# One copy of the bias rows for both halves, byte masks, later small loads, and an output in pieces

## The chip, the cores and the metric

The kernel runs on one core of a Trainium2 chip. The metric is device time in microseconds for one execution. Before the change the median of three runs is 849.18 us (849.12 to 850.76). All engine times below come from one further execution, recorded by the hardware profiler: it took 852.8 us, of which 851.0 us lie between its first and its last instruction (the span).

The engines are PE (TensorE, the matmuls), DVE (VectorE), ACT (ScalarE), POOL (GpSimd) and SP (SyncE, which here only issues DMAs).

## The reference, cut to what matters

Two blocks run on 256 tokens of width 1024 (16 "meta" tokens stand ahead of them in the first block, which makes 272 rows).

```python
a = rms_norm(h, norm_mix)
(q_na, k_na, v_na, q_hg, z_f, z_b, i_hg, g_hg, gate_na, gate_hg) = split_cols(a @ w_in)
y_na  = neighbourhood_attention(q_na, k_na, v_na, rpb) @ w_na_out     # 8 heads, bias table rpb (8 x 15 x 31)
y_hg  = hgrn2_branch(q_hg, z_f, z_b, i_hg, g_hg, lb, hg_norm) @ w_hg_out   # two gated scans
h = h + (sigmoid(gate_na) * y_na + sigmoid(gate_hg) * y_hg) @ w_o
h = h + square(relu(rms_norm(h, norm_mlp) @ w_up)) @ w_down
x = rms_norm(h, norm_final)[:, 16:]
# second block, two layers:
ada = silu(c) @ ada_w + ada_b                 # shift, scale, gate; ada_w is 1024 x 3072 per layer
x = x + gate * ((mixers of (rmsnorm(x) * (1 + scale) + shift) @ in_w) * silu(gate2)) @ out_w
out = rmsnorm(x, final_g)                     # 256 x 1024
```

In the neighbourhood attention a grid row of 64 tokens sees a window of 16 columns, and the bias of a query and a key is an entry of `rpb` that depends on their distance alone. The scans use seven binary masks of 128 x 128 (`lvl`).

## The kernel before

All weights are fp32 and are multiplied in three passes: a weight is split into a rounded high part and the rest. Weights come in 129 "units" of 512 x 512 (1 MB), in the order in which PE uses them: `gh` (units 0 and 1), `kn` (2 and 3), `qn` (4 and 5), `vn` (6 and 7) and so on. `emit_raw` loads a unit (L222, on SP's queue) into one of three `raw` buffers. `emit_hl` splits it in two halves: ACT writes `whi` (L252), DVE then writes `wlo` = raw - whi (L253, two SBUF inputs). There are six pairs of half-unit buffers. A raw buffer is free again when DVE has split its second half; a `whi`/`wlo` pair is free when PE has read it last.

PE accumulates in four PSUM banks (`acc`). `gh` uses two. `kn` uses four, one for each 128 columns (L357 to L359), and `qn` uses the same four again: qn's first matmul can start only when the first of kn's results has been copied out of its bank (`ev_kn`: ACT L647 or DVE L649, and a last DVE copy L651).

`bias_loads` builds the bias of the attention for two halves of the grid. For each half four DMAs (L622) fetch rows of `rpb` into a tile `braw`, and 12 additions on POOL (L627) add the window mask, which lies in `cs` (a constant, loaded at L584); both inputs lie in SBUF. `lvf` (448 KB of fp32, L586) is cast to bytes by POOL (L587) to give the masks `lvl`. `ada()` loads `ada_w` in 48 pieces of 512 KB (L457, issued by POOL) into four slots and multiplies them on DVE (L473, two operations each). At the end `ev_oo` normalizes the last rows: half by ACT (L1648), half by DVE (L1650), each with its own output DMA.

A scheduler that runs ahead of time with its own model of costs sets the order of the instructions on each engine. `with after(x):` tells it to issue what follows behind x. Each queue executes its instructions in that order; an instruction that waits holds all behind it on its engine.

Of the kernel before, what the change touches and what calls it, by code (L numbers as in the profile page):

```python
# [7 lines left out]
F32 = mybir.dt.float32  # L8
# [3 lines left out]
AF = mybir.ActivationFunctionType  # L12
ALU = mybir.AluOpType
# [14 lines left out]


C_LV = 0  # L30
C_ID = 896
C_WIN = C_ID + 128
C_GLA = C_WIN + 80
C_CUM = C_GLA + 128
# [7 lines left out]
def consts():  # L42
    import numpy as np

    c = np.zeros((128, C_N), np.float32)
    p = np.arange(128)
    c[:, C_ID:C_ID + 128] = np.eye(128)
    for i in range(7):

        a, b = p[:, None] >> i, p[None, :] >> i  # L50
        c[:, 128 * i:128 * i + 128] = (a ^ b) == 1
    for hf in (0, 1):
        col = 32 * hf + 31 - p % 32
        key = 24 * hf + np.arange(40)
        s = np.clip(col - 8, 0, 48)
        ok = (key[None, :] >= s[:, None]) & (key[None, :] < s[:, None] + 16)
        c[:, C_WIN + 40 * hf:C_WIN + 40 * hf + 40] = np.where(ok, 0.0, -1e30)
    t = np.arange(128)

    c[:, C_GLA:C_GLA + 128] = p[:, None] <= t[None, :]  # L60

    c[:, C_CUM:C_CUM + 128] = ((p[:, None] <= t[None, :]) & (p[:, None] // 64 == t[None, :] // 64)) / 16.0
    for g, w in enumerate((2, 4, 8, 16)):
        c[:, C_RC + 16 * g:C_RC + 16 * g + 16] = 1.0 / np.minimum(np.arange(16) + 1, w)
    return c
# [3 lines left out]
def kernel(  # L69
# [5 lines left out]
    vecs, cst, out, dbg=None,  # L75
):
    nc = tc.nc
    V, S, T, G = nc.vector, nc.scalar, nc.tensor, nc.gpsimd
# [17 lines left out]
    def mt(i, shape, dt=F32, name="m"):  # L96
        return slot.tile(shape, dt, name=nm(name), tag=f"m{i}")
# [33 lines left out]
    cs = cp.tile([128, C_N - C_WIN], F32, name="cs")  # L131
    lvl = cp.tile([128, 896], U8, name="lvl")
    vrow = cp.tile([128, 128], F32, name="vrow")
    vc = cp.tile([128, 128], F32, name="vc")
    h = [cp.tile([128, D], F32, name=f"h{t}") for t in range(2)]
# [67 lines left out]
            add_units(("oo", j, n), odd_out_w, 512 * j, 512 * n)  # L203

    raw_t, hl_t = {}, {}
    borrowed = {}
    cap = [1 << 30]
    BORROW = {("v0", 0): (("m8", "m9"), ("m10", "m11")), ("v0", 1): (("l0", "l1"), ("l2", "m18")),
# [5 lines left out]
    def emit_raw(n):  # L214
        while st["raw"] < min(n, len(units)):
            i = st["raw"]
            t = rawp.tile([128, 2048], F32, name=nm("raw"), tag="raw")
            src = units[i][1]
            d = t.rearrange("p (k n) -> p k n", n=src.shape[2])

            for k in (slice(0, 2), slice(2, 4)) if i < QD else (slice(None),):
                nc.sync.dma_start(out=d[:, k], in_=src[:, k])  # L222
            raw_t[i] = t
            st["raw"] += 1


    for key, tags in BORROW.items():
        i = [u[0] for u in units].index(key)
# [43 lines left out]
    def after(instructions):  # L272
        es = ExitStack()
        for ins in instructions:
            es.enter_context(tc.issue_after(ins.ins))
        return es
# [169 lines left out]
    def ada(l, js, slots):  # L446
        if 4 in js:
            gr[l] = mt(13 + l, [128, D], name="gr")
        parts = [(j, k2) for j in js for k2 in range(4)]
        ws = []  # L450

        def load(i):

            if i < len(parts):
                j, k2 = parts[i]
                w = slot.tile([128, 2, 512], F32, name=nm("adw"), tag=slots[i % len(slots)])
                nc.gpsimd.dma_start(out=w, in_=ada_w[l, 256 * k2:256 * k2 + 256, 512 * j:512 * j + 512]  # L457
                                    .rearrange("(k p) n -> p k n", p=128))
                ws.append(w)

        for i in range(len(slots)):
            load(i)
        i = len(slots)
        yield 3000
        for j in js:
            a = tb()
            G.memset(a, 0.0)
            nc.gpsimd.dma_start(out=a[0:1], in_=ada_b[l:l + 1, 512 * j:512 * j + 512])
            for k2 in range(4):
                w = ws.pop(0)  # L470
                for k in range(2):
                    kk = 2 * k2 + k
                    V.scalar_tensor_tensor(out=a, in0=w[:, k], scalar=csil[:, kk:kk + 1], in1=a,  # L473
                                           op0=ALU.mult, op1=ALU.add)
                load(i)
                i += 1
                yield 1200
            if j < 4:

                p2 = transposes(a).rearrange("p (k c) -> p k c", k=4)  # L480
                if j < 2:
                    V.tensor_reduce(out=cols[:, l, 8 + 4 * j:12 + 4 * j], in_=p2, axis=AX.X, op=ALU.add)
                else:

                    o = R_NG + 8 * l + 4 * (j - 2)
                    c = small([128, 4])
                    V.tensor_reduce(out=c, in_=p2, axis=AX.X, op=ALU.add)
                    V.scalar_tensor_tensor(out=cols[:, l, 4 * (j - 2):4 * (j - 2) + 4], in0=c, scalar=1.0,
                                           in1=vc[:, o:o + 4], op0=ALU.add, op1=ALU.mult)
            else:  # L490
                ps = mps()

                ah, al = tb(dt=F32R), tb(dt=F32R)
                split_bank(a, ah, al)
                T.matmul(ps, lhsT=ones_r, rhs=ah, start=True, stop=False)
                T.matmul(ps, lhsT=ones_r, rhs=al, start=False, stop=True)
                S.activation(out=gr[l][:, 512 * (j - 4):512 * (j - 4) + 512], in_=ps, func=AF.Copy)
            yield 100
# [77 lines left out]
    def ev_gh(t, ps):  # L576
# [4 lines left out]

    xstat_unit([("gh", 0), ("gh", 1)], xT, ev_gh)
    meta_in()
    nc.sync.dma_start(out=cs, in_=cst[:, C_WIN:])  # L584
    lvf = mt(8, [128, 896], name="lvf")
    nc.sync.dma_start(out=lvf, in_=cst[:, 0:896])  # L586
    G.tensor_copy(out=lvl, in_=lvf)  # L587
    pv = mps()
    T.transpose(out=pv[:, 0:128], in_=vrow, identity=ident)
    V.tensor_copy(out=vc, in_=pv[:, 0:128])  # L590
# [4 lines left out]
                    in0=vc[:, R_LB:R_LB + 16].rearrange("p (d l h) -> p d l h", d=2, l=2)[:, :, 0],  # L595
                    in1=vc[:, R_LB:R_LB + 16].rearrange("p (d l h) -> p d l h", d=2, l=2)[:, :, 1], op=ALU.subtract)
# [16 lines left out]
    bias = [lt(hf, [128, 8, 176], name=f"bias{hf}") for hf in range(2)]  # L613

    def bias_loads():
        for hf in range(2):
            raw = mt(10 + hf, [128, 8, 133], name="braw")
            for r in range(4):

                src = bass.AP(tensor=na_rpb.tensor, offset=na_rpb.offset + (7 - r) * 31 - 16 - 8 * hf,  # L620
                              ap=[[1, 32], [465, 8], [1, 133]])
                nc.sync.dma_start(out=raw[32 * r:32 * r + 32], in_=src)  # L622
            for hd in range(8):
                rv = raw[:, hd]
                for r0, n, o in KEYS[hd // 2 % 2][:-1]:
                    rows = bass.AP(tensor=rv.tensor, offset=rv.offset + 31 * r0, ap=[list(rv.ap[0]), [31, n], [1, 40]])
                    G.tensor_tensor(out=bias[hf][:, hd, o:o + 40 * n].rearrange("p (j c) -> p j c", j=n), in0=rows,  # L627
                                    in1=C(C_WIN + 40 * hf, 40).unsqueeze(1).to_broadcast([128, n, 40]), op=ALU.add)
                o = KEYS[hd // 2 % 2][-1]
                G.memset(bias[hf][:, hd, o:o + 16], 0.0)  # L630
            yield 0
# [372 lines left out]
    for n in range(2):  # L1004
        ws = use(("yn", n))
        for t in range(2):
# [3 lines left out]
            c = slice(512 * n, 512 * n + 512)  # L1010
# [3 lines left out]
    for n in range(2):  # L1014
        ws = use(("yh", n))
        nl = len(later)
        for t in range(2):
# [3 lines left out]
            c = slice(512 * n, 512 * n + 512)  # L1021
# [333 lines left out]
    for t in range(2):  # L1355
        for gp in range(2):
            ps = mps()
            for k in range(2):
                g = 2 * gp + k
                for c in range(2):  # L1360
                    i = 2 * g + c
# [121 lines left out]
    GA = {}  # L1483

    glw = cp.tile([128, 8, 16], F32, name="glw")
    nc.sync.dma_start(out=glw, in_=odd_in_w[:, 2048:2064].rearrange("(k p) n -> p k n", p=128))
    glr = cp.tile([128, 8, 32], F32R, name="glr")
    split_bank(glw, glr[:, :, 0:16], glr[:, :, 16:32])
    gw3 = slot.tile([33, 512], F32, name="gw3", tag="c0")
    nc.sync.dma_start(out=gw3[0:16], in_=gla_gate_w)  # L1490
    nc.sync.dma_start(out=gw3[16:32], in_=gla_gate_w)
    nc.sync.dma_start(out=gw3[32:33], in_=gla_gate_b)

    def gla_gate():
        pg = mps()
# [145 lines left out]
    def ev_oo(t, n, ps, a, b):  # L1641
        c = slice(512 * n + a, 512 * n + b)
        resid(1, t, n, ps, a, b)
        if n == 0:
            G.tensor_tensor(out=h[t][:, c], in0=h[t][:, c], in1=fg_b[:, c], op=ALU.mult)
        if n == 1 and b == 512:
            r = rpow(sqs[t])
            S.activation(out=h[t][:, 0:512], in_=h[t][:, 0:512], func=AF.Copy, scale=r)  # L1648
            nc.scalar.dma_start(out=out[128 * t:128 * t + 128, 0:512], in_=h[t][:, 0:512])
            V.scalar_tensor_tensor(out=h[t][:, 512:1024], in0=h[t][:, 512:1024], scalar=r, in1=fg_b[:, 512:1024],  # L1650
                                   op0=ALU.mult, op1=ALU.mult)
            nc.sync.dma_start(out=out[128 * t:128 * t + 128, 512:1024], in_=h[t][:, 512:1024])

    out_proj("oo", (2, 3, 0, 1), oT, ev_oo, halves=True)

# [44 lines left out]
```

## Time and profile before

| what | value |
|---|---|
| median of three runs | 849.18 us |
| the profiled execution | 852.8 us, span 851.0 us |
| PE busy | 829.6 us (97%) |
| DVE, ACT, POOL busy | 585.4, 463.9, 89.7 us |
| bytes read from HBM | 167.00 MB, 197 GB/s over the span |
| mean granted clock of PE | 0.996 |

A line of the timeline reads: start, duration (of the whole group where it says x2 or more), engine, source line, operation, result <- operands, shapes, and in brackets the idle time of the engine ahead of it with what ended it. A matmul's duration is longer than the distance to the next one, since matmuls overlap; the distance of two starts tells PE's pace.

### The profile page before, as it was taken

The numbers are of one execution on the slowest core, as the hardware profiler recorded it, in microseconds if no ns is written. First come the engines' busy times: TensorE is split into PE (matmuls) and PEld (weight loads), VectorE is DVE, ScalarE is ACT, GpSimd is POOL, SyncE is SP. The second block draws the span as 40 slices with busy tenths as digits, with TensorE's granted clock in tenths as the row PEclk, the third lists the DMA queues.
The fourth block names the chain that finished last, engine by engine and source line by source line (L and its number), as shares of the span: only waits on it lengthen the run. The fifth ranks groups of instructions, "written<-read, shape, count | busy, mean of one in ns | idle before, by whom it ended". The sixth has DMA issues, their size and how long they took to land.

```text
span 851.0 us, 12884 instructions
## 1 busy us (share of the span) xinstructions
PE 829.6 (97%) x5037; PEld 735.7 (86%) x5037; DVE 585.4 (69%) x838; ACT 463.9 (55%) x757; POOL 89.7 (11%) x188
## 2 busy tenths in 40 slices
PE   7799999999999999999999999999999999999996
PEld 4799998888889999999878988888789999888885
DVE  6756668764858887767976768966655557568743
ACT  6356755564557545545766545554566455455442
POOL 2400020001002221102021001100000000031001
PEclk9999999999999999999999999999999999999999
DMA  9874344441648998858737657856155445559611
GB/s 274 234 246 140 110 149 148 147 150 53 217 152 309 369 359 297 297 196 282 245 119 247 191 169 229 281 196 238 60 202 176 154 151 176 161 196 314 191 62 49
DMA packets 82832, 168.87 MB, mean 198 GB/s; under 512 B 4770, under 2 KB 9250, under 8 KB 82772
## 3 DMA queue, kind: packets, MB, share of 16 engines
q1 hardware_dynamic: 75188, 142.34, 49.8%
q0 software_dynamic: 7296, 25.19, 8.6%
q8 instruction: 39, 0.64, 0.3%
q10 hardware_dynamic: 288, 0.52, 0.2%
q14 instruction: 21, 0.17, 0.1%
HBM read 167.00 MB, written 1.05 MB: 197 GB/s over the span
## 4 chain that ended last, share of the span: by engine, by line
PE 90%; DVE 4%; DMA 2%; ACT 1%; issue 1%; POOL 0%; SPq 0%; POOLq 0%; ACTq 0%; DVEq 0%
PE acc L349 16%; PE acc L347 16%; PE acc L348 16%; PE acc L359 7%; PE acc L358 7%; PE acc L357 7%; PE mp L359 3%; PE mp L357 3%; PE mp L358 3%; PE mp L406 3%; DVE wlo L253 2%; PE mp L869 1%; DMA raw<-in_w_in_dram 1%; DMA h<-in_x_dram 1%; ACT junk L438 1%
## 5 line engine op out<-in xcount | busy, mean ns | idle before, releaser
L253 DVE TENSOR_TENSOR wlo<-raw,whi 128x1024 fp32r<-128x1024 f32 x244 | 297.7, 1240 | 136.2 <-ACT whi L252 133.8
L252 ACT ACTIVATE whi<-raw 128x1024 fp32r<-128x1024 f32 x244 | 251.2, 1055 | 170.0 <-PE acc L349 88.1
L473 DVE SCALAR_TENSOR_TENSOR tb<-adw,csil,tb 128x512 f32<-128x512 f32 x96 | 71.0, 747 | 8.2 <-DMA tb<-in_ada_b_dram 5.2
L359 PE MATMUL acc<-xh,wlo 128*128 128x272 f32 (+1 forms) x224 | 65.0, 292 | 4.6 <-DVE wlo L253 4.6
L358 PE MATMUL acc<-xl,whi 128*128 128x272 f32 (+1 forms) x224 | 65.1, 291 | 0.0
L357 PE MATMUL acc<-xh,whi 128*128 128x272 f32 (+1 forms) x224 | 64.9, 291 | 0.0
L357 PE MATMUL mp<-uh,whi 128*128 128x256 f32 x224 | 63.3, 284 | 0.0
L358 PE MATMUL mp<-ul,whi 128*128 128x256 f32 x224 | 63.2, 283 | 0.0
L359 PE MATMUL mp<-uh,wlo 128*128 128x256 f32 x224 | 62.3, 283 | 0.0
L457 POOL DMA_DIRECT2D adw<-in_ada_w_dram x48 | 35.2, 733 | 198.3 <-DVE tb L473 118.7
L359 PE MATMUL acc<-oh,wlo 128*128 128x256 f32 x192 | 55.0, 287 | 0.0
L358 PE MATMUL acc<-ol,whi 128*128 128x256 f32 x192 | 54.6, 284 | 0.0
L357 PE MATMUL acc<-oh,whi 128*128 128x256 f32 x192 | 54.4, 283 | 0.0
L347 PE MATMUL acc<-whi,hh 128*128 128x512 f32 x128 | 49.9, 391 | 0.0
L348 PE MATMUL acc<-wlo,hh 128*128 128x512 f32 x128 | 49.8, 390 | 0.0
L349 PE MATMUL acc<-whi,hl 128*128 128x512 f32 x128 | 49.7, 389 | 0.0
L347 PE MATMUL acc<-whi,yT 128*128 128x512 f32 (+1 forms) x128 | 48.5, 379 | 0.0
L348 PE MATMUL acc<-wlo,yT 128*128 128x512 f32 (+1 forms) x128 | 48.3, 378 | 0.0
L349 PE MATMUL acc<-whi,yT 128*128 128x512 f32 (+1 forms) x128 | 48.3, 377 | 0.0
L359 PEld LDWEIGHTS acc<-xh,wlo 128*128 128x128 f32 x224 | 42.6, 191 | 4.8 <-DVE wlo L253 4.8
L348 PE MATMUL acc<-wlo,oh 128*128 128x512 f32 x112 | 44.5, 398 | 0.0
L347 PE MATMUL acc<-whi,oh 128*128 128x512 f32 x112 | 44.2, 395 | 0.0
(415 smaller groups left out, 2053.2 us busy)
## 6 DMA issues: line engine op xcount, KB each, us to landing
raw<-in_odd_in_w_dram SPq DMA_DIRECT2D x28, 1024.0 KB, 5.2
adw<-in_ada_w_dram POOLq DMA_DIRECT2D x48, 512.0 KB, 6.2
raw<-in_w_in_dram SPq DMA_DIRECT2D x21, 1024.0 KB, 5.2
raw<-in_even_in_w_dram SPq DMA_DIRECT2D x20, 1024.0 KB, 5.2
raw<-in_w_up_dram SPq DMA_DIRECT2D x16, 1024.0 KB, 7.4
raw<-in_w_down_dram SPq DMA_DIRECT2D x16, 1024.0 KB, 8.5
raw<-in_even_out_w_dram SPq DMA_DIRECT2D x8, 1024.0 KB, 5.1
raw<-in_odd_out_w_dram SPq DMA_DIRECT2D x8, 1024.0 KB, 5.2
```

The source lines that it names most:

```text
L252: S.activation(out=hi.rearrange("p k n -> p (k n)"), in_=r, func=AF.Copy)
L253: V.tensor_tensor(out=lo.rearrange("p k n -> p (k n)"), in0=r, in1=f(hi.rearrange("p k n -> p (k n)")), op=ALU.subtract)
L347: T.matmul(ps, lhsT=xh, rhs=wh, start=first and k == 0, stop=False)
L348: T.matmul(ps, lhsT=xh, rhs=wl, start=False, stop=False)
L349: last_mm[:] = [T.matmul(ps, lhsT=xl, rhs=wh, start=False, stop=last and k == n - 1)]
L357: T.matmul(ps, lhsT=wh[:, c], rhs=xh, start=first and k == 0, stop=False)
L358: T.matmul(ps, lhsT=wh[:, c], rhs=xl, start=False, stop=False)
L359: T.matmul(ps, lhsT=wl[:, c], rhs=xh, start=False, stop=last and k == n - 1)
L406: last_t[:] = [T.transpose(out=ps[:, 128 * b:128 * b + 128], in_=src[:, 128 * b:128 * b + 128], identity=ident)]
L438: S.activation(out=j[0:src.shape[0], 0:n], in_=src, func=AF.Square, scale=float(of or n) ** -0.5, accum_out=a)
L457: nc.gpsimd.dma_start(out=w, in_=ada_w[l, 256 * k2:256 * k2 + 256, 512 * j:512 * j + 512] .rearrange("(k p) n -> p k n", p=128))
L473: V.scalar_tensor_tensor(out=a, in0=w[:, k], scalar=csil[:, kk:kk + 1], in1=a, op0=ALU.mult, op1=ALU.add)
```

## The change

1. The seven masks are stored as bytes in the constant and are loaded straight into `lvl` (112 KB instead of 448 KB). POOL's cast is gone.
2. The bias rows are loaded once for both halves: one tile for heads 0 to 3 and one for heads 4 to 7, each of four DMAs of 32 x 4 x 141 numbers (72 KB) in place of 32 x 8 x 133 (133 KB). The 24 additions stay the same, but half 0 now reads both tiles, and so does half 1; all 12 additions that read the first tile can stand ahead of the others.
3. The loads of `cs`, the bias rows, `lvl`, `glw` and `gw3` are issued behind the last weight load that was emitted before them (`after(raw_ins)`).
4. The 48 loads of `ada_w` go on SP's queue instead of POOL's.
5. DVE's half of the last output is computed and stored in two pieces of 256 columns.

```diff
-C_ID = 896
+C_ID = 224
...
+    masks = np.zeros((128, 896), np.uint8)
...
-        c[:, 128 * i:128 * i + 128] = (a ^ b) == 1
+        masks[:, 128 * i:128 * i + 128] = (a ^ b) == 1
+    c[:, C_LV:C_LV + 224] = masks.view(np.float32)
...
-                nc.sync.dma_start(out=d[:, k], in_=src[:, k])
+                raw_ins[:] = [nc.sync.dma_start(out=d[:, k], in_=src[:, k])]
...
-                nc.gpsimd.dma_start(out=w, in_=ada_w[l, 256 * k2:256 * k2 + 256, 512 * j:512 * j + 512]
+                nc.sync.dma_start(out=w, in_=ada_w[l, 256 * k2:256 * k2 + 256, 512 * j:512 * j + 512]
...
-    nc.sync.dma_start(out=cs, in_=cst[:, C_WIN:])
-    lvf = mt(8, [128, 896], name="lvf")
-    nc.sync.dma_start(out=lvf, in_=cst[:, 0:896])
-    G.tensor_copy(out=lvl, in_=lvf)
+
+    with after(raw_ins):
+        nc.sync.dma_start(out=cs, in_=cst[:, C_WIN:])
...
+        raw = [mt(10 + i, [128, 4, 141], name="braw") for i in range(2)]
+        with after(raw_ins):
+            for i in range(2):
+                for r in range(4):
+                    src = bass.AP(tensor=na_rpb.tensor, offset=na_rpb.offset + 4 * 465 * i + (7 - r) * 31 - 24,
+                                  ap=[[1, 32], [465, 4], [1, 141]])
+                    nc.sync.dma_start(out=raw[i][32 * r:32 * r + 32], in_=src)
+            nc.sync.dma_start(out=lvl.bitcast(F32), in_=cst[:, C_LV:C_LV + 224])
         for hf in range(2):
-            raw = mt(10 + hf, [128, 8, 133], name="braw")
-            for r in range(4):
-
-                src = bass.AP(tensor=na_rpb.tensor, offset=na_rpb.offset + (7 - r) * 31 - 16 - 8 * hf,
-                              ap=[[1, 32], [465, 8], [1, 133]])
-                nc.sync.dma_start(out=raw[32 * r:32 * r + 32], in_=src)
             for hd in range(8):
-                rv = raw[:, hd]
+                rv = raw[hd // 4][:, hd % 4, 8 - 8 * hf:]
...
-            V.scalar_tensor_tensor(out=h[t][:, 512:1024], in0=h[t][:, 512:1024], scalar=r, in1=fg_b[:, 512:1024],
-                                   op0=ALU.mult, op1=ALU.mult)
-            nc.sync.dma_start(out=out[128 * t:128 * t + 128, 512:1024], in_=h[t][:, 512:1024])
+            for k in range(2):
+
+                c = slice(512 + 256 * k, 768 + 256 * k)
+                V.scalar_tensor_tensor(out=h[t][:, c], in0=h[t][:, c], scalar=r, in1=fg_b[:, c],
+                                       op0=ALU.mult, op1=ALU.mult)
+                nc.sync.dma_start(out=out[128 * t:128 * t + 128, c], in_=h[t][:, c])
```

The scheduler makes a new order out of this. At the start of the program SP issues its loads so before the change (raw_227 is unit 3, raw_312, raw_374 and raw_448 are units 4, 5 and 6):

```order
L574 DMA hgn_b<-in_hg_norm_dram 128x512
L584 DMA cs<-in_cst_dram 128x400
L586 DMA lvf_291<-in_cst_dram 128x896
L622 DMA braw_483<-in_na_rpb_dram 32x8x133
L622 DMA braw_458<-in_na_rpb_dram 32x8x133 x2
L622 DMA braw_483<-in_na_rpb_dram 32x8x133
L622 DMA braw_458<-in_na_rpb_dram 32x8x133
L622 DMA braw_483<-in_na_rpb_dram 32x8x133
L622 DMA braw_458<-in_na_rpb_dram 32x8x133
L222 DMA raw_227<-in_w_in_dram 128x4x512
L622 DMA braw_483<-in_na_rpb_dram 32x8x133
L1486 DMA glw<-in_odd_in_w_dram 128x8x16
```

And so after it (raw_309, raw_371, raw_445 and raw_558 are units 4, 5, 6 and 7; braw_455 holds heads 0 to 3):

```order
L578 DMA hgn_b<-in_hg_norm_dram 128x512
L226 DMA raw_227<-in_w_in_dram 128x4x512
L590 DMA cs<-in_cst_dram 128x400
L226 DMA raw_309<-in_w_in_dram 128x4x512
L226 DMA raw_371<-in_w_in_dram 128x4x512
L226 DMA raw_445<-in_w_in_dram 128x4x512
L627 DMA braw_455<-in_na_rpb_dram 32x4x141 x4
L627 DMA braw_456<-in_na_rpb_dram 32x4x141 x4
L628 DMA lvl<-in_cst_dram 128x224
L226 DMA raw_558<-in_w_in_dram 128x4x512
```

Unit 3 has moved ahead of `cs`, the masks and the bias rows, and the bias rows have moved behind unit 6; `glw` stands some 70 loads later.

DVE's rows at the same place, before (wlo_230 and wlo_234 are unit 3, wlo_315 to wlo_381 units 4 and 5; kT is kn's result leaving the PSUM banks):

```order
L253 TENSOR_TENSOR wlo_230<-raw_227,whi_229 128x1024
L253 TENSOR_TENSOR wlo_234<-raw_227,whi_233 128x1024
L414 TENSOR_TENSOR glr<-glw,glr 128x8x16
L579 SCALAR_TENSOR_TENSOR gg_190<-gg_190,acc_194 128x512
L580 TENSOR_TENSOR gg_190<-gg_190,hgn_b 128x512
L253 TENSOR_TENSOR wlo_315<-raw_312,whi_314 128x1024
L253 TENSOR_TENSOR wlo_319<-raw_312,whi_318 128x1024
L253 TENSOR_TENSOR wlo_377<-raw_374,whi_376 128x1024
L253 TENSOR_TENSOR wlo_381<-raw_374,whi_380 128x1024
L649 COPY kT_311<-acc_323 128x40 x2
L651 COPY kT_311<-acc_322 128x2x16
```

And after (wlo_230 and wlo_234 stand ten rows further up; wlo_312 and wlo_316 are unit 4, wlo_374 and wlo_378 unit 5):

```order
L257 TENSOR_TENSOR wlo_312<-raw_309,whi_311 128x1024
L583 SCALAR_TENSOR_TENSOR gg_190<-gg_190,acc_194 128x512
L257 TENSOR_TENSOR wlo_316<-raw_309,whi_315 128x1024
L584 TENSOR_TENSOR gg_190<-gg_190,hgn_b 128x512
L257 TENSOR_TENSOR wlo_374<-raw_371,whi_373 128x1024
L257 TENSOR_TENSOR wlo_378<-raw_371,whi_377 128x1024
L658 COPY kT_308<-acc_319 128x2x16
L656 COPY kT_308<-acc_320 128x40 x2
```

In both orders the two splits of unit 5 stand directly ahead of the copies that free kn's banks for qn.

At the start of the MLP, where the first `ada_w` pieces are used (tb is their accumulator), DVE's rows before are (wlo_2625 to wlo_2637 are units 34 and 35, wlo_2643 unit 36):

```order
L253 TENSOR_TENSOR wlo_2625<-raw_2527,whi_2624 128x1024
L253 TENSOR_TENSOR wlo_2629<-raw_2527,whi_2628 128x1024
L253 TENSOR_TENSOR wlo_2633<-raw_2529,whi_2632 128x1024
L253 TENSOR_TENSOR wlo_2637<-raw_2529,whi_2636 128x1024
L473 SCALAR_TENSOR_TENSOR tb_2798<-adw_2651,csil,tb_2798 128x512
L253 TENSOR_TENSOR wlo_2643<-raw_2640,whi_2642 128x1024
```

and after (wlo_2623 to wlo_2635 are units 34 and 35):

```order
L257 TENSOR_TENSOR wlo_2623<-raw_2525,whi_2622 128x1024
L257 TENSOR_TENSOR wlo_2627<-raw_2525,whi_2626 128x1024
L257 TENSOR_TENSOR wlo_2631<-raw_2527,whi_2630 128x1024
L477 SCALAR_TENSOR_TENSOR tb_2796<-adw_2649,csil,tb_2796 128x512
L257 TENSOR_TENSOR wlo_2635<-raw_2527,whi_2634 128x1024
L257 TENSOR_TENSOR wlo_2641<-raw_2638,whi_2640 128x1024
```

The first product of `ada_w` has moved ahead of the second split of unit 35.

## Rows read from the trace of the kernel before

**Rows 1.** Page, part 1: busy us of each engine (share of the span), instructions.
```profile
PE 829.6 (97%) x5037; PEld 735.7 (86%) x5037; DVE 585.4 (69%) x838; ACT 463.9 (55%) x757; POOL 89.7 (11%) x188
```

**Rows 2.** PE's waits: engine line <- what it waited for: total us, times, longest.
```profile
PE acc L359 <- DVE wlo L253: 4.6, 1, 4.6
PE mp L510 <- DMA grow<-in_vecs_dram: 3.3, 1, 3.3
PE acc L347 <- ACT xh L413: 3.0, 1, 3.0
```

**Rows 3.** Windows: length, busy us (count) PE, PEld, DVE, ACT, POOL, clock, DMA share, GB/s.
```profile
20.00:40.00 20.00, 15.43 (x94) 13.82 (x93) 14.78 (x22) 6.48 (x12) 10.46 (x26) 0.91 0.87 222
...
260.00:280.00 20.00, 20.00 (x137) 18.58 (x137) 18.41 (x22) 12.89 (x20) 2.99 (x5) 1.00 1.02 382
```

**Rows 4.** Chain that ended last, first 40 us: start, us, what.
```profile
14.25 2.35 DVE wlo L253 x2
...
21.30 7.84 DMA raw<-in_w_in_dram
29.17 1.07 ACT whi L252
30.26 5.75 DVE wlo L253
```

**Rows 5.** Timeline of PE, 20 to 46 us.
```profile
26.80 0.29 PE L358 MATMUL acc<-xl,whi 128*128 128x272 f32 x1
...
31.20 0.29 PE L358 MATMUL acc<-xl,whi 128*128 128x272 f32 x1
36.06 0.60 PE L359 MATMUL acc<-xh,wlo 128*128 128x272 f32 x1 [4.57 <-DVE wlo L253]
...
39.11 0.29 PE L358 MATMUL acc<-xl,whi 128*128 128x272 f32 x1
...
44.78 0.28 PE L357 MATMUL acc<-xh,whi 128*128 128x256 f32 x1
```

**Rows 6.** Timeline of POOL, 20 to 46 us.
```profile
26.43 8.49 POOL L627 TENSOR_TENSOR bias<-braw,cs 128x160 f32<-128x160 f32 x24 [3.16 <-DMA braw<-in_na_rpb_dram]
```

**Rows 7.** Timeline of SP's queue, 8 to 46 us.
```profile
9.44 0.34 SPq L574 DMA_DIRECT2D hgn_b<-in_hg_norm_dram  x1
...
13.92 5.02 SPq L622 DMA_DIRECT2D braw<-in_na_rpb_dram  x7
```

**Rows 8.** DMA from 8 to 46 us: GB/s in 40 slices; an issue's count, KB, us to landing.
```profile
GB/s 407 390 408 392 298 286 371 383 390 391 227 162 140 175 201 173 228 208 313 369 228 216 291 369 392 379 371 216 41 15 0 24 144 395 407 239 138 386 405 401
...
hgn_b<-in_hg_norm_dram SPq DMA_DIRECT2D x1, 256.0 KB, 8.3
```

**Rows 9.** Page, part 6: DMA issues of the whole run, count, KB each, median us to landing.
```profile
adw<-in_ada_w_dram POOLq DMA_DIRECT2D x48, 512.0 KB, 6.2
raw<-in_w_in_dram SPq DMA_DIRECT2D x21, 1024.0 KB, 5.2
```

**Rows 10.** Timeline of DVE, 20 to 46 us.
```profile
21.50 0.67 DVE L414 TENSOR_TENSOR xl<-mp,xh 128x512 fp32r<-128x512 f32 x1
...
38.58 4.62 DVE L253 TENSOR_TENSOR wlo<-raw,whi 128x1024 fp32r<-128x1024 f32 x4
...
43.34 0.18 DVE L651 COPY kT<-acc 128x32 f32<-128x32 f32 x1
```

**Rows 11.** Start of the MLP: timeline of POOL.
```profile
257.11 2.99 POOL L457 DMA_DIRECT2D adw<-in_ada_w_dram  x4 [5.15 <-PE mp L349]
```

**Rows 12.** Start of the MLP: timeline of DVE.
```profile
262.93 0.75 DVE L473 SCALAR_TENSOR_TENSOR tb<-adw,csil,tb 128x512 f32<-128x512 f32 x1 [0.24 <-DMA adw<-in_ada_w_dram]
```

**Rows 13.** Start of the MLP: timeline of PE.
```profile
266.32 0.28 PE L359 MATMUL mp<-uh,wlo 128*128 128x256 f32 x1
```

**Rows 14.** Timeline of the end, all engines, 842 to 851 us.
```profile
845.27 0.72 ACT L1648 ACTIVATE h<-h,sm 128x512 f32<-128x512 f32 x1 [0.86 <-POOL sm L430]
845.27 0.75 DVE L1650 SCALAR_TENSOR_TENSOR h<-h,sm,fg_b 128x512 f32<-128x512 f32 x1 [0.67 <-POOL sm L430]
```

More of the change, by code (lines that the diff above doesn't have):

```diff
@@ L205 @@
     raw_t, hl_t = {}, {}
+    raw_ins = []
     borrowed = {}
@@ L1485 @@
     glw = cp.tile([128, 8, 16], F32, name="glw")
-    nc.sync.dma_start(out=glw, in_=odd_in_w[:, 2048:2064].rearrange("(k p) n -> p k n", p=128))
+    with after(raw_ins):
+        nc.sync.dma_start(out=glw, in_=odd_in_w[:, 2048:2064].rearrange("(k p) n -> p k n", p=128))
     glr = cp.tile([128, 8, 32], F32R, name="glr")
@@ L1489 @@
     gw3 = slot.tile([33, 512], F32, name="gw3", tag="c0")
-    nc.sync.dma_start(out=gw3[0:16], in_=gla_gate_w)
-    nc.sync.dma_start(out=gw3[16:32], in_=gla_gate_w)
-    nc.sync.dma_start(out=gw3[32:33], in_=gla_gate_b)
+    with after(raw_ins):
+        nc.sync.dma_start(out=gw3[0:16], in_=gla_gate_w)
+        nc.sync.dma_start(out=gw3[16:32], in_=gla_gate_w)
+        nc.sync.dma_start(out=gw3[32:33], in_=gla_gate_b)
     def gla_gate():
@@ L1647, in ev_oo @@
             r = rpow(sqs[t])
-            S.activation(out=h[t][:, 0:512], in_=h[t][:, 0:512], func=AF.Copy, scale=r)
-            nc.scalar.dma_start(out=out[128 * t:128 * t + 128, 0:512], in_=h[t][:, 0:512])
-            V.scalar_tensor_tensor(out=h[t][:, 512:1024], in0=h[t][:, 512:1024], scalar=r, in1=fg_b[:, 512:1024],
-                                   op0=ALU.mult, op1=ALU.mult)
-            nc.sync.dma_start(out=out[128 * t:128 * t + 128, 512:1024], in_=h[t][:, 512:1024])
+            c = slice(0, 512)
+            S.activation(out=h[t][:, c], in_=h[t][:, c], func=AF.Copy, scale=r)
+            nc.scalar.dma_start(out=out[128 * t:128 * t + 128, c], in_=h[t][:, c])
+            for k in range(2):
[3 more added lines that the diff above has]
+                nc.sync.dma_start(out=out[128 * t:128 * t + 128, c], in_=h[t][:, c])
     out_proj("oo", (2, 3, 0, 1), oT, ev_oo, halves=True)
```

## The prediction

> **What bounds the kernel now.** The busy times come first: PE works 829.6 of 851.0 us [rows 1], so a change gains only what PE waits for or what lies before its first and behind its last matmul. PE's list of waits, read next, has one long wait behind the start: 4.6 us for a DVE split [rows 2]. The other two long ones belong to the first 11 us, before any weight is multiplied, where the change moves nothing that they wait for. The windows place the wait: in 20 to 40 us PE is busy for 15.43 us and its granted clock is 0.91, while later windows are full at 1.00 [rows 3].
>
> The chain of waits tells the story of that stretch [rows 4]: unit 3 was issued at 21.30 us and took 7.84 us, ACT's half of the split 1.07 us, DVE's half 5.75 us. In PE's timeline [rows 5] kn's matmuls run from 26.80 to 31.20 us in 35 steps, 0.126 us each; then nothing starts until 36.06; from there 13 steps to 39.11 take 3.05 us in place of 13 x 0.126 = 1.64 us, the half-rate level (1.2 of 2.4 GHz) in the granted clock. The idle time is 36.06 - 31.20 - 0.126 = 4.73 us, and the slow restart costs 1.41 us. qn's first matmul follows at 44.78 us.
>
> Why did one split take 5.75 us when four in a row take 4.62 us, 1.16 us each [rows 10]? POOL ran its 24 bias additions from 26.43 to 34.92 us [rows 6]. The split was free to start at 30.26 us, and ended at 36.01 us, 1.09 us behind the last addition. DVE stood still until POOL had finished its whole series, although each addition lasts only 8.49 / 24 = 0.35 us. Both have two SBUF inputs. So PE's stall has two parents: a late unit 3, and a bias series that keeps DVE out.
>
> The Trainium skill ("SBUF — State Buffer", Who interferes with whom) says that such a DVE instruction and a GpSimd instruction that reads SBUF share a port pair, and that whoever is first holds it for the whole instruction. By that rule alone the split would have lost one addition, 0.35 us, and not the series; the row shows the series, and the sum goes by the row. The rule taken by the instruction is rival B below.
>
> **The change, part by part.** *Unit 3 moves ahead of the small loads.* It waits now only for the raw buffer of unit 0, which is free at about 14.3 us, when DVE turns to unit 1's splits at 14.25 [rows 4]. It stands behind hgn_b, which lands at 9.44 + 8.3 = 17.74 us [rows 7, 8]. In busy slices the DMA moves about 390 GB/s [rows 8], so 1 MB takes 2.7 us: unit 3 lands at 20.45 us, 8.7 us earlier than before (21.30 + 7.84 = 29.14). DVE splits it behind the copy that began at 21.50 [rows 10], first half at about 22.2, second half done at about 24.7 us, before kn starts. PE's stall at 31.2 us is gone. Without a further wait kn (96 matmuls, all now behind gh, from 26.55 us) ends at 26.55 + 96 x 0.126 = 38.65 us; qn would start 44.78 - 38.65 = 6.13 us earlier. That is the whole prize, 4.73 + 1.41 us.
>
> *The bias rows move behind unit 6.* Units 4 and 5 wait for the buffers of units 1 and 2 (free at 14.25 + 2.35 = 16.6 and at 21.5 us) [rows 4, 10]. Behind unit 3 and cs (200 KB, 0.5 us) unit 4 lands at 20.45 + 0.5 + 2.7 = 23.65 us; unit 5 takes the 5.2 us of a single load [rows 9] from 21.5 us: 26.7 us. Unit 6 waits for unit 3's second split, is issued at 24.7 and lands at 29.9 us. Four bias DMAs follow. Before, seven were issued over 5.02 us, 0.72 us apart [rows 7]; the new ones have half the packets, so I take 0.36 us each. By bytes alone (72 KB at 390 GB/s) it is 0.19 us, and at the old spacing 0.72 us. The first tile is complete at W = 29.9 + 4 x 0.36 = 31.3 us (30.6 to 32.7). POOL starts there. The second tile has 4.2 us more and does not hold it up. The series lasts 8.49 us as before, until W + 8.49 = 39.8 us.
>
> What is late next is unit 5. Its first half needs the buffers of unit 2's first half, which PE reads last with kn's 42nd matmul: 26.55 + 42 x 0.126 = 31.85 us, plus the end of that matmul and ACT's 1.07 us, about 33.2 us. Then POOL has been running for 2 us, and DVE is kept out until 39.8. Queued on DVE behind it are unit 5's second half and the copies that free kn's first PSUM bank, for which qn waits. From the end of the series: 1.09 us for the split that waited [rows 4, 6], 1.16 us for the next, 0.18 us for copy L651 [rows 10]: 42.2 us. PE ends kn at 38.65, idles for 3.6 us, and I charge the slow restart again, 1.41 us, since the only stall of such length in mid-stream was followed by it. Net: 44.78 - 42.2 - 1.4 = 1.15 us gained. With W at its two ends it is 1.85 or -0.25 us; without a slow restart 1.4 us more.
>
> *Behind that stretch* POOL ends 4.9 us later than before, but the bias is first read with the attention's scores, on the far side of qn and vn (12 us each). vn's splits have qn's 12 us, and from 40 to 60 us PE waited for no split before: its list of waits [rows 2] has one only.
>
> *Bytes instead of fp32 masks, fewer bias bytes.* 336 KB and 8 x 61 KB less, 2.1 us of DMA time; already counted in the landing times above. POOL's cast goes from an idle POOL: 0. Bounds: 0 to -0.3 us.
>
> *ada_w on SP's queue.* 48 issues leave POOL; SP gets them. No piece stands ahead of a weight load that would be free earlier than it. PE does not wait in 260 to 280 us although the DMA is full (382 GB/s) [rows 3]; the bytes stay the same. I take 0; the price if the cover goes is rival D.
>
> *glw and gw3 later:* their splits move to stretches in which DVE and ACT are idle now and then; 0, at most +0.3 us.
>
> *Output in pieces.* DVE's half takes 0.75 us and ACT's 0.72 us, both from 845.27 [rows 14]; each is followed by a DMA of its 256 KB. DVE's first piece leaves some 0.35 us earlier, the second at the same time as before, and ACT's whole half no earlier at all: 0, between -0.3 and +0.2 us.
>
> Sum against the profiled execution: 852.8 - 1.15 = 851.65 us. It lay 3.6 us above the median of the runs, so against the median: 849.18 - 1.15 = 848.0 us.
>
> **Rivals.** *B, the whole prize.* If DVE gets in between two additions, or if the bias rows land later than 34.4 us so that both splits of unit 5 are over, nothing holds qn: -6.1 us, 843.1 us. For it: the rule named above in its plain reading, since an addition lasts 0.35 us. Against it: the 5.75 us of the split [rows 4], and 34.4 lies 1.7 us above the upper bound of W.
>
> *C, slower: the series falls between the two splits of unit 5.* If W lies between 33.2 and 34.35 us, the first split runs and the additions take over behind it, until 34.3 + 8.5 = 42.8; the second split and the copy follow, qn starts at 44.1, and with 1.4 us of slow clock that is 45.5 against 44.78: +0.75 us, 849.9 us. It decides from 33.2 us on, 0.5 us above W's upper bound. For it: DMAs behind one another spread more than my sum does.
>
> *D, ada_w's first piece holds a split.* DVE's first product now stands ahead of the second split of unit 35, which PE first reads at about 266.3 us [rows 13]; with 0.75 us [rows 12] and 1.16 us ahead of that, the piece must land by 264.4 us. It is issued about 257.5 us [rows 11]; at the median of 6.2 us [rows 9] it lands at 263.7. At 8.5 us it is 1.6 us late, which eats case A's gain: +0.5 us, 849.7 us.
>
> *E, nothing.* Unit 3 lands no earlier, since something else than its buffer holds it, or what is won is lost at once: 849.2 us. Against it: nothing else stands before it on SP's queue but hgn_b.
>
> **How the numbers follow.** A (the stall moves to qn's start, 846.6 to 849.4 us): 0.62; B: 0.16; C: 0.10; D: 0.05; E: 0.07. What can be told from no change here is about 0.2%, 1.7 us. A counts as faster where the bias rows come early or the clock stays up, which I give 0.24 of its 0.62; with B that makes 0.40. Slower by over 1.7 us needs C or D together with the upper bounds of the small terms: 0.08. The rest, 0.52, is within 0.2%. The range goes from B's 843.1 to C's 849.9 with 0.3 us for the small terms: 843.0 to 850.2; A's own is 846.6 to 849.4.
>
> **What would show it.** In the new profile PE's wait for L253 at 31 us should be gone, and the chain should show unit 3 landing near 20.5 us. POOL's 24 additions should start at 31.3 us and last 8.5 us; one wlo inside should last 6 us or more, and PE should wait some 3.6 us at the start of qn for a copy of kn, with the granted clock below 1.00 in 40 to 60 us. If that wlo lasts 1.2 us and PE goes through, B is right. If two wlo stand on both sides of the series, C. If PE waits at 266 us for a wlo, D. A wait of PE in another place, above all in the MLP, would make the whole sum wrong.

## The result, and the profile after

The changed kernel takes 845.15 us (median of 4 runs, 844.54 to 846.2), the kernel before beside it 849.91 us. The ratio is 0.9948, with a 95% interval from 0.9929 to 0.9967: 0.52% or 4.4 us faster. The prediction said 848.0 us within 843.0 to 850.2: the range holds it, but the gain is about four times the 1.15 us forecast, and it is made of other parts. The changed kernel's profiled execution took 845.33 us, its span is 843.4 us.

Busy times (columns as in [rows 1]) and PE's waits of the changed kernel:

```profile
PE 828.1 (98%) x5037; PEld 734.7 (87%) x5037; DVE 581.4 (69%) x840; ACT 464.4 (55%) x757; POOL 59.2 (7%) x139
```

```profile
PE mp L514 <- DMA grow<-in_vecs_dram: 3.3, 1, 3.3
PE acc L351 <- ACT xh L417: 3.1, 1, 3.1
PE mp L410 <- DVE xn L1228: 1.0, 2, 0.5
```

The wait for L253 (now L257) that headed [rows 2] is gone; the two waits of the first 11 us are the same. The windows (length, busy us and count of PE, PEld, DVE, ACT, POOL, granted clock, DMA share, GB/s) are full where [rows 3] had 15.43 us and a clock of 0.91:

```profile
20.00:40.00 20.00, 20.00 (x141) 18.53 (x140) 15.20 (x36) 10.39 (x18) 7.46 (x14) 1.00 0.87 274
40.00:60.00 20.00, 20.00 (x166) 20.00 (x166) 10.51 (x12) 10.05 (x19) 7.92 (x12) 1.00 0.55 179
```

PE's timeline, kn's first matmuls and qn's first one (compare [rows 5]):

```profile
26.91 0.41 PE L361 MATMUL acc<-xh,whi 128*128 128x272 f32 x2
...
38.99 0.28 PE L361 MATMUL acc<-xh,whi 128*128 128x256 f32 x1
```

From kn's first matmul to qn's first one it takes 38.99 - 26.91 = 12.08 us: 96 steps of 0.126 us without a stop. POOL's series and DVE's splits of unit 5 show why no new stall came at qn. First POOL's timeline (compare [rows 6]), then DVE's:

```profile
33.50 14.42 POOL L634 TENSOR_TENSOR bias<-braw,cs 128x160 f32<-128x160 f32 x24 [10.77 <-DMA braw<-in_na_rpb_dram]
```

```profile
33.53 3.00 DVE L257 TENSOR_TENSOR wlo<-raw,whi 128x1024 fp32r<-128x1024 f32 x2 [2.92 <-ACT whi L256]
36.45 0.18 DVE L658 COPY kT<-acc 128x32 f32<-128x32 f32 x1
...
39.90 2.84 DVE L257 TENSOR_TENSOR wlo<-raw,whi 128x1024 fp32r<-128x1024 f32 x2
```

The series began 0.03 us ahead of the split, and this time DVE was not shut out: two splits took 3.00 us in place of the 2.35 us of [rows 4], while POOL's 24 additions took 14.42 us in place of 8.49. In the single records an addition with a split beside it lasts 1.24 to 1.49 us, and a split beside an addition 1.29 to 1.56 us. In this stretch the two engines take turns, one instruction each, and the copy L658 was done at 36.6 us, 2.4 us before qn needed the bank.

SP's queue shows the early unit 3 (14.50 us, where [rows 4] has 21.30) and the bias rows behind unit 6:

```profile
14.50 0.37 SPq L226 DMA_DIRECT2D raw<-in_w_in_dram  x1
14.91 0.51 SPq L590 DMA_DIRECT2D cs<-in_cst_dram  x1
16.77 8.40 SPq L226 DMA_DIRECT2D raw<-in_w_in_dram  x3
25.22 7.54 SPq L627 DMA_DIRECT2D braw<-in_na_rpb_dram  x8
```

The second place that moved is the end, which the prediction held for worthless. From the start of the last matmul to the end of the span it took 851.0 - 842.55 = 8.45 us before and 843.4 - 836.41 = 7.0 us after. PE's last matmul, before and then after:

```profile
842.55 0.28 PE L349 MATMUL mp<-whi,yT 128*128 128x256 f32 x1
```

```profile
836.41 0.28 PE L353 MATMUL mp<-whi,yT 128*128 128x256 f32 x1
```

At the kernel's last line the profile has rows called DRAIN for every engine, and rows on which the engines wait for each other. These are the drains of POOL and SP, before and after (count, then ns min/median/max, then first and last start):

```profile
L1696 POOLq DRAIN  x3: 46/102/5583, 844.6 to 850.8; - x3
L1696 SPq DRAIN  x3: 7/7/7, 849.1 to 850.5; - x3
```

```profile
L1709 POOLq DRAIN  x3: 46/98/1656, 838.5 to 843.2; - x3
L1709 SPq DRAIN  x3: 7/7/7, 842.6 to 842.9; - x3
```

POOL's first drain took 5.58 us from 844.65, until 850.23 us, although SP, which waits for the last output, drained at 849.1. So POOL ended last, 1.1 us behind SP. After the change it takes 1.66 us and is over 2.4 us before SP.

### The profile page after: what moved, and what is told of

Its sections match the earlier page's. It is cut to its first block, busy times and chain, and to the rows that moved or that the text cites. A ratio compares the mean times of both kernels' runs of the same rounds, so it can differ in the third digit from the quotient of the medians.

```text
span 843.4 us, 12871 instructions
## 1 busy us (share of the span) xinstructions
PE 828.1 (98%) x5037; PEld 734.7 (87%) x5037; DVE 581.4 (69%) x840; ACT 464.4 (55%) x757; POOL 59.2 (7%) x139
## 3 DMA queue, kind: packets, MB, share of 16 engines
HBM read 166.14 MB, written 1.05 MB: 198 GB/s over the span
## 4 chain that ended last, share of the span: by engine, by line
PE 93%; DVE 2%; DMA 1%; ACT 1%; issue 1%; POOL 0%; SPq 0%; POOLq 0%; DVEq 0%; ACTq 0%
PE acc L351 17%; PE acc L353 17%; PE acc L352 16%; PE acc L362 7%; PE acc L363 7%; PE acc L361 7%; PE mp L363 3%; PE mp L362 3%; PE mp L361 3%; PE mp L410 3%; PE mp L876 1%; DMA h<-in_x_dram 1%; ACT junk L442 1%; PE mp L353 1%; PE mp L351 1%
## 5 line engine op out<-in xcount | busy, mean ns | idle before, releaser
L257 DVE TENSOR_TENSOR wlo<-raw,whi 128x1024 fp32r<-128x1024 f32 x244 | 295.0, 1226 | 140.9 <-ACT whi L256 138.5
L352 PE MATMUL acc<-wlo,eh 128*128 128x512 f32 x112 | 44.0, 393 | 0.0
L353 PE MATMUL acc<-whi,ol 128*128 128x512 f32 x112 | 43.9, 392 | 0.0
```

The source lines that it names most:

```text
L257: V.tensor_tensor(out=lo.rearrange("p k n -> p (k n)"), in0=r, in1=f(hi.rearrange("p k n -> p (k n)")), op=ALU.subtract)
L352: T.matmul(ps, lhsT=xh, rhs=wl, start=False, stop=False)
L353: last_mm[:] = [T.matmul(ps, lhsT=xl, rhs=wh, start=False, stop=last and k == n - 1)]
```

## The experiments

**The kernel before, three more traces.** No edit; `e1` has eleven timed runs, the other two are single executions.

> The kernel before, unchanged, for a second trace and for the spread of its time. Theory T (a split that comes while the bias additions run is shut out for the rest of the series): the first split of unit 3 again lasts 5 to 6 us, POOL's series 8.5 us, PE waits 4.5 to 5 us at 31 us. Rival R (the two engines take turns, one instruction each, as in the changed kernel's trace, and the 5.75 us were one accident of timing): the split lasts 1.2 to 1.6 us, POOL's series 9.5 us or more, PE waits under 1 us there, and the span is some 3 us or more under 851.0 us. Either way the ratio to the kernel before is 1.000 within 0.002.

Measured: 849.23 us, ratio 1.0003 [0.9994, 1.0012], span 847.7. Its trace is not the one on which the prediction stands. PE's waits in kn and qn's first matmul, then POOL, then DVE:

```profile
32.31 0.39 PE L359 MATMUL acc<-xh,wlo 128*128 128x272 f32 x1 [0.27 <-DVE wlo L253]
33.74 0.39 PE L359 MATMUL acc<-xh,wlo 128*128 128x272 f32 x1 [0.41 <-DVE wlo L253]
34.85 0.39 PE L357 MATMUL acc<-xh,whi 128*128 128x272 f32 x1 [0.46 <-DVE gg L579]
41.42 0.35 PE L357 MATMUL acc<-xh,whi 128*128 128x256 f32 x1
```

```profile
26.37 15.48 POOL L627 TENSOR_TENSOR bias<-braw,cs 128x160 f32<-128x160 f32 x24 [2.80 <-DMA braw<-in_na_rpb_dram]
```

```profile
30.81 2.88 DVE L253 TENSOR_TENSOR wlo<-raw,whi 128x1024 fp32r<-128x1024 f32 x2 [3.78 <-ACT whi L252]
```

```profile
20.00:40.00 20.00, 18.86 (x125) 16.73 (x124) 14.54 (x25) 8.56 (x16) 16.09 (x24) 1.00 0.94 256
```

Rival R: two splits in 2.88 us, POOL stretched to 15.48 us, three waits that sum to 1.14 us, the clock at 1.00, qn at 41.42 us. The theory of the shut-out falls for this execution. The third wait, for `gg`, has the same root as the other two: in DVE's order before the change `gg` stands behind unit 3's splits.

> The kernel before, unchanged, a third trace. Theory T (the 5.75 us split is a rare case; most executions look like the second trace): splits inside POOL's series last 1.2 to 1.6 us, the series 13 us or more, qn starts at 41 to 43 us, time 847.5 to 850.5 us. Rival S (the two cases are about as frequent): a split of 4 us or more, qn at 44 us or later, time 852 us or more, in this or the next trace.

> The kernel before, unchanged, a fourth trace; theories as in the third: T says 1.2 to 1.6 us for each split in the series, S says a split of 4 us or more in one of the two.

The third and the fourth trace are of the same kind, theory T: 848.45 and 848.23 us, POOL's series 15.40 and 15.35 us, the splits of unit 3 below. qn starts at 40.30 and 40.14 us, earlier than the 41 to 43 us expected.

```profile
29.91 2.67 DVE L253 TENSOR_TENSOR wlo<-raw,whi 128x1024 fp32r<-128x1024 f32 x2 [3.52 <-ACT whi L252]
```

```profile
29.53 2.69 DVE L253 TENSOR_TENSOR wlo<-raw,whi 128x1024 fp32r<-128x1024 f32 x2 [3.05 <-ACT whi L252]
```

So the 5.75 us of [rows 4] came once in four traces of this kernel. It is likely rarer among the timed runs: that execution took 852.8 us, and the 65 runs of the kernel before that were timed beside the first two sets of experiments and as `e1` lie between 847.07 and 851.55 us. They have no traces, so a shorter stall of the same kind can't be excluded in the slowest of them.

**Only the order of the first loads (`e2`).** Kernel before, with

```diff
+                raw_ins[:] = [nc.sync.dma_start(out=d[:, k], in_=src[:, k])]
...
+    with after(raw_ins):
+        nc.sync.dma_start(out=cs, in_=cst[:, C_WIN:])
+        nc.sync.dma_start(out=lvf, in_=cst[:, 0:896])
...
+                with after(raw_ins):
+                    nc.sync.dma_start(out=raw[32 * r:32 * r + 32], in_=src)
```

(lines taken out are not shown).

> The kernel before with one part of the change: cs, lvf and the bias rows are issued behind the last weight load, so that unit 3 is loaded early; fp32 masks, two copies of the bias rows, ada_w on POOL's queue and the undivided output stay. Theory T (the early unit 3 is what moved PE): PE's wait at 31 us is gone and kn to qn runs through, 3 to 6 us less in the time, most of what the whole change gave. Rival S (the smaller loads made the room): the 1.5 MB of small loads push unit 4, 5 or 6 late, PE waits 1 us or more in qn or vn, and less than half of the change's gain is seen.

Measured: 846.92 us, ratio 0.9973 [0.9964, 0.9982], 2.3 us faster. PE is full from 20 us on:

```profile
20.00:40.00 20.00, 20.00 (x141) 18.51 (x140) 14.78 (x36) 10.26 (x18) 3.24 (x4) 1.00 1.04 294
```

The direction is theory T's; the size (2.3 us, half of the whole change) is below the 3 to 6 us that it expected, since the waits that are to be had in a usual execution are those of `e1`: qn starts at 39.13 us, 2.3 us before `e1`. This run moves both parents of the stall, since POOL's additions began only at 39.21 us; the next two runs take them apart.

**Only the additions later (`e3`).** Kernel before, with the mask in a tile of its own that is loaded behind unit 6 (`raw_ins` set as in the run above):

```diff
+        csw = cp.tile([128, 80], F32, name="csw")
+        with after(raw_ins):
+            nc.sync.dma_start(out=csw, in_=cst[:, C_WIN:C_WIN + 80])
...
-                                    in1=C(C_WIN + 40 * hf, 40).unsqueeze(1).to_broadcast([128, n, 40]), op=ALU.add)
+                                    in1=csw[:, 40 * hf:40 * hf + 40].unsqueeze(1).to_broadcast([128, n, 40]), op=ALU.add)
```

> The kernel before, where only POOL's 24 additions are moved: their mask is read from a second small tile that is loaded behind unit 6, so they start near 43 us. Unit 3 is as late as before. Theory T (both parents are needed for the long wait: a late unit 3 and DVE kept out): unit 3 lands at 29.1 us, ACT 1.07, DVE 1.2, ready at 31.4 to 31.5 us, PE waits 0.1 to 0.4 us, kn ends within 0.5 us of its unhindered time, 4 to 6 us less than before. Rival S (the late load alone makes PE wait): PE still waits over 2 us at 31 us and under half of the gain is seen.

Measured: 848.43 us, ratio 0.9993 [0.9984, 1.0002]: no change that can be told. No addition ran beside the splits of units 3 to 5 (POOL began at 40.72 us), and PE waits all the same:

```profile
32.09 0.39 PE L359 MATMUL acc<-xh,whi 128*128 128x272 f32 x1 [0.22 <-ACT whi L254]
33.35 0.39 PE L361 MATMUL acc<-xh,wlo 128*128 128x272 f32 x1 [0.74 <-DVE wlo L255]
35.28 0.46 PE L359 MATMUL acc<-xh,whi 128*128 128x272 f32 x1 [0.15 <-DVE gg L581]
```

```profile
20.00:40.00 20.00, 18.76 (x109) 16.35 (x109) 13.59 (x25) 8.48 (x16) 1.83 (x2) 0.91 1.04 268
```

The waits shown sum to 1.1 us, as in `e1`, and here the clock fell to 0.91. Unit 3 was issued 1.2 us later than in `e1` in this trace (22.27 us), and the trace is that of the slowest of the eleven runs (850.84 us), so the two do not compare cleanly; but a late unit 3 makes PE wait without any addition beside it, and taking the additions away alone buys nothing. Theory T's gain of 4 to 6 us did not come. Rival S is right that the late load alone makes PE wait, though its 2 us or more did not come either.

**Only smaller loads (`e7`).** Kernel before with byte masks and one copy of the bias rows, `raw_ins` left empty so that `after` orders nothing:

```diff
-                raw_ins[:] = [nc.sync.dma_start(out=d[:, k], in_=src[:, k])]
+                nc.sync.dma_start(out=d[:, k], in_=src[:, k])
```

(that line against the changed kernel; the output in one piece and `ada_w` on POOL's queue as before).

> The kernel before with byte masks and one copy of the bias rows, and without the order behind the weights (ada_w on POOL's queue, one output piece). Unit 3 stands behind the eight bias loads, which are half as long. Theory T (the order is needed): unit 3 lands only some 3 to 4 us earlier than 29 us and its split meets POOL's series; gain at most half of that of the early unit 3 alone (2.2 us). Rival S (smaller loads are enough): PE does not wait at 31 us, and the time falls by 2 us or more.

Measured: 847.58 us, ratio 0.9980 [0.9971, 0.9990], 1.7 us faster. Unit 3 was issued at 19.98 us, and of PE's waits there 0.04 us are left:

```profile
20.00:40.00 20.00, 19.96 (x138) 18.17 (x137) 16.57 (x35) 10.08 (x19) 14.71 (x25) 1.00 0.90 295
```

Unit 3 was issued only 0.3 us earlier than in `e9` (20.29 us), but it landed 3.5 us earlier. ACT's split, which waits for it, in `e9` and then here:

```profile
28.82 2.01 ACT L252 ACTIVATE whi<-raw 128x1024 fp32r<-128x1024 f32 x2 [4.00 <-DMA raw<-in_w_in_dram]
```

```profile
25.34 2.01 ACT L256 ACTIVATE whi<-raw 128x1024 fp32r<-128x1024 f32 x2 [2.34 <-DMA raw<-in_w_in_dram]
```

From its issue that is 5.4 us in place of 8.5. Theory T's landing 3 to 4 us earlier came, its wait did not: nearer to rival S (2 us or more), the smaller loads alone take away the wait too, with POOL's series (20.70 to 34.52 us) beside all the splits. So an early landing of unit 3 is what `e2` and this run have in common. The order and the smaller loads are two ways to the same gain. They do not add: the changed kernel with `ada_w` on POOL (`e4`, next) has both, and its ratio is that of the order alone.

**`ada_w` back on POOL's queue (`e4`).** Changed kernel, with

```diff
-                nc.sync.dma_start(out=w, in_=ada_w[l, 256 * k2:256 * k2 + 256, 512 * j:512 * j + 512]
+                nc.gpsimd.dma_start(out=w, in_=ada_w[l, 256 * k2:256 * k2 + 256, 512 * j:512 * j + 512]
```

> The changed kernel with ada_w's 48 loads back on POOL's queue. Theory T (POOL's drain at the end of the program takes longer the more DMAs POOL has issued: 1.66 us in the changed kernel, 5.58 us before): the drain is again 5 us or more, the program ends some 1.1 us later behind the last output's landing, and the time is 0.8 to 1.3 us longer than the changed kernel's. Rival S (the queue costs nothing, as the prediction said): drain and end as in the changed kernel, within 0.3 us of its time.

Measured: 846.97 us, ratio to before 0.9977 [0.9969, 0.9986], where the changed kernel has 0.9948 [0.9929, 0.9967] and 0.9954 [0.9941, 0.9968] (`e11`): 2 to 2.5 us of the gain are lost by these ratios. Theory T expected 0.8 to 1.3 us, which these intervals do not exclude; the spans differ by 844.8 - 843.4 = 1.4 us. POOL's drain is back at its old length:

```profile
L1709 POOLq DRAIN  x3: 46/93/5583, 838.5 to 844.5; - x3
```

From the last matmul to the end it takes 8.5 us again, although the output is in pieces.

**Only `ada_w` on SP's queue (`e6`).** Kernel before, with the reverse of that line.

> The kernel before with one part of the change: ada_w's 48 loads on SP's queue. Theory T (POOL's drain at the end ends last before, 5.58 us from its start): the drain falls to about 1.7 us, the tail behind the last matmul from 8.46 to 7.3 or 7.4 us, the time by 1.0 to 1.6 us (the middle of the program may add 0.3 to 0.5). Rival S (the queue is worth nothing by itself; what the changed kernel lost without it came from how it collides with other loads): within 0.5 us of the kernel before.

Measured: 847.91 us, ratio 0.9979 [0.9970, 0.9987], 1.8 us faster [1.1 to 2.5]. POOL's drain takes 1651 ns, and the end takes 846.4 - 839.01 = 7.4 us:

```profile
839.01 0.28 PE L349 MATMUL mp<-whi,yT 128*128 128x256 f32 x1
```

The end gives 8.45 - 7.4 = 1.05 us, as theory T has it; PE waits in kn as in `e1` (0.9 us for two splits, 0.5 us for gg). Where the rest of the 1.8 came from, if it is real, is open. A part may lie between 420 and 440 us, where PE is busy for 19.32 us in this trace and for 18.75 in `e1`'s; but two traces of the changed kernel, at 19.03 and 18.74 us, differ by half as much there.

**The output in one piece (`e5`).** Changed kernel with the old `ev_oo`.

```diff
-            for k in range(2):
-
-                c = slice(512 + 256 * k, 768 + 256 * k)
...
+            V.scalar_tensor_tensor(out=h[t][:, 512:1024], in0=h[t][:, 512:1024], scalar=r, in1=fg_b[:, 512:1024],
+                                   op0=ALU.mult, op1=ALU.mult)
+            nc.sync.dma_start(out=out[128 * t:128 * t + 128, 512:1024], in_=h[t][:, 512:1024])
```

> The changed kernel with DVE's half of the last output in one piece, as before. Theory T (with ada_w off POOL's queue the end of the program waits for SP, which waits for the last output's landing): SP's last drain comes 6.55 us behind the last matmul in place of 6.2, the program 0.2 to 0.5 us longer. Rival S (the pieces bought the end): 1.0 us or more longer, and tail (last matmul to end) 8.0 us or more in place of 7.0.

Measured: 845.41 us, ratio 0.9953 [0.9939, 0.9966]; in time it can't be told from the changed kernel. In the trace the end takes 7.4 us, 0.4 us more than with pieces, as theory T expected.

**Each addition three times (`e8`).** Changed kernel; its time says nothing here, since the attention then waits for POOL (2.7 us in its trace).

```diff
-                for r0, n, o in KEYS[hd // 2 % 2][:-1]:
+                for r0, n, o in KEYS[hd // 2 % 2][:-1] * 3:
```

> The changed kernel, where POOL does each bias addition three times (72 in a row, the same result), to see more meetings of DVE's splits with the series. Theory T (they take turns, one instruction each, unless DVE comes within some 0.04 us ahead of POOL's next addition): nearly all splits last 1.2 to 1.6 us with one addition stretched beside each; a split shut out for two or more additions comes only where DVE started 0.04 us or less ahead of an addition. Rival S (a running series shuts DVE out): splits of 3 us or more, many of them, at any distance. The attention may start later, since the bias is ready later; the time is not compared.

Measured: the series ran from 33.95 to 70.87 us, and none of the 12 splits beside it lasted more than 1.6 us. The longest pair:

```profile
50.96 2.96 DVE L257 TENSOR_TENSOR wlo<-raw,whi 128x1024 fp32r<-128x1024 f32 x2 [3.45 <-ACT whi L256]
```

Three of them came within 0.04 us ahead of POOL's next addition; each let one addition pass, and no more. Theory T holds in this stretch, apart from its guess that such a split may lose two or more.

**The changed kernel again, and without any large use of POOL's queue (`e11`, `e12`).** `e12` moves the 12 loads of `ada_b` to SP as well:

```diff
-            nc.gpsimd.dma_start(out=a[0:1], in_=ada_b[l:l + 1, 512 * j:512 * j + 512])
+            nc.sync.dma_start(out=a[0:1], in_=ada_b[l:l + 1, 512 * j:512 * j + 512])
```

> The changed kernel again, to be compared with the next one on the same chip: 844.5 to 846.2 us, ratio to before 0.993 to 0.997; PE's busy time in 20 to 60 us full, tail 7.0 us, POOL's drain 1.65 us.

> The changed kernel with the last 12 DMAs of POOL's queue (ada_b, 2 KB each) on SP's too. Theory T (POOL's drain grows with the DMAs that POOL has issued, (5.58 - 1.65) / 48 = 0.082 us each, and ends last only above some 4 us): the drain falls to 0.6 to 0.7 us and the time stays within 0.3 us of the changed kernel's, since SP ends last by 2 us already. Rival S (any DMA on POOL's queue costs at the end): 0.5 us or more faster.

Measured: `e11` 845.35 us, ratio 0.9954 [0.9941, 0.9968]; `e12` 844.42 us, ratio 0.9945 [0.9932, 0.9957]. Its drain:

```profile
L1709 POOLq DRAIN  x3: 34/82/656, 838.2 to 842.9; - x3
```

The drain is 0.66 us as expected, and the end is no shorter (7.0 us). Its median is the lowest of all kernels here, 0.9 us under the changed kernel on the same chip, but the intervals overlap; whether it is faster is not settled.

## Why the prediction was right in direction and wrong in its steps

*The prize was mis-sized.* The step that "qn would start 44.78 - 38.65 = 6.13 us earlier" rests on one execution. Against that trace qn did start 44.78 - 38.99 = 5.8 us earlier, but the other traces of the same kernel have qn at 41.42, 40.30 and 40.14 us: 1.2 to 2.4 us to be gained, not 6.1. The sum named the warning itself (the profiled execution lay 3.6 us above the median) and then subtracted a stall of that execution from the median.

*"DVE stood still until POOL had finished its whole series" was read as a rule; it was one case.* In 13 traces of all the kernels since, 81 splits met POOL's additions, and the longest took 1.60 us. The Trainium skill ("SBUF — State Buffer", SBUF: two separate sides) says that whichever of the two engines starts first has the shared port pair for the whole instruction, and that the other is fully blocked. Turns of one instruction each are what these traces show, with up to 1.58 us for an addition that had to let a split of 1.2 us pass. I set that rule aside for one row, and the row was the exception.

*Case A therefore failed at "Then POOL has been running for 2 us, and DVE is kept out until 39.8".* The bias rows landed later than my upper bound (POOL began at W = 33.50 us, not 30.6 to 32.7). Unit 6 was issued at 24.80 us, as forecast; from there to W it took 8.7 us in place of 5.2 + 4 x 0.36 = 6.6. Bytes were not the limit: from 31.5 to 33.5 us the DMA moved 26 GB/s. My sum counted four loads behind unit 6, and eight were issued there; that these and unit 6 hold each other up is likely and was not tested. That W lies in the window of rival C, but the series did not take over behind the first split. What happened is rival B's mechanism: DVE got in between two additions and PE ran through. B's 843.1 us was too low, since it too took 6.1 us from the median.

*"Unit 3 lands at 20.45 us" and "PE's stall at 31.2 us is gone" held* (ACT began to split it at 20.72 us), and `e2` shows that the order alone gives 2.3 us. The smaller loads, costed at 0 beyond that, are worth 1.7 us by themselves and next to nothing behind the order. No run takes the later `glw` and `gw3` by themselves, nor the masks without the bias rows.

*"`ada_w` on SP's queue: I take 0" was wrong.* PE indeed never waited in the MLP, and rival D did not come: the first product began at 256.34 us with a wait of 0.56 us. But POOL's drain at the end was in the way, and the sum had looked for the end among the output's DMAs alone. The drain takes 5.58 us in all traces with 60 DMAs on POOL's queue, 1.65 us with 12 and 0.66 us with none: (5.58 - 0.66) / 60 = 0.082 us each. The number counts and not the bytes: the 48 loads of 512 KB add (5.58 - 1.65) / 48 = 0.082 us each, the 12 of 2 KB (1.65 - 0.66) / 12 = 0.083 us. Before, it ended 1.1 us behind SP.

*"Output in pieces: 0" held only while POOL's drain covered it.* Behind the shorter drain the pieces take 0.4 us off the end in the trace.

Together, against the trace `e1`, whose time (849.5 us) is near the medians: its span of 847.7 us less 843.4 us is 4.3 us. The last matmul's way to the end gives 1.45 us of it; in the first 45 us qn comes 41.42 - 38.99 = 2.4 us earlier; the rest, under 0.5 us, lies behind 400 us, where the order of DVE's work differs, and was not traced further. This is the gain that was timed, 4.4 us. Against `e9` and `e10`, which are faster than the medians, the spans give 3.2 and 3.0 us, of which the end has the same 1.45 us and qn's earlier start 1.3 and 1.2 us.

That the time fell inside the range is therefore in part luck: case A, which had most of the chance, did not happen, the prize was at most 2.4 us where the sum had 6.1, and 1.45 us came from two terms that the sum put at nothing.

What stays open: why the split in the first trace lost thirteen turns. It came 0.02 us ahead of an addition (single records give the distances here). Seven other splits came within 0.05 us of the next one, at 0.003, 0.007, 0.018, 0.021, 0.031, 0.041 and 0.043 us; five let one addition pass and two none. The distance alone doesn't decide it.

## What to carry to other kernels

A stall that the profile shows once is a case, not a price: when the profiled execution lies well above the median, ask for a second trace of the same kernel, or for the part of it that the median can't hold, before you subtract it. Look at what each engine still does behind its last useful instruction: a queue that was used throughout can cost its time at the very end. And two edits that remove the same wait are worth one of them.

## What the runs showed of the hardware that was not expected

POOL's drain at the end of the program grows with the number of DMAs that POOL issued, large or small: 0.66, 1.65 and 5.58 us for 0, 12 and 60. DVE's splits and POOL's additions, each with two SBUF inputs, take turns when they meet, so the longer instruction sets the pace of both: 24 additions stretch from 8.49 us to 12.5 to 15.5 us, while a DVE split loses at most 0.4 us. Once, in 82 meetings, one split waited for thirteen additions. And waits of PE between 32 and 36 us went with a granted clock of 0.91 from 20 to 40 us in one trace (`e3`, 1.1 us of waits) and of 1.00 in three others (`e9` 0.9, `e1` 1.1, `e6` 1.4 us).
